# Second branch's operand loaded in the first three dilated items, minimum over key halves by one operand, last memory gating behind the last shift

## Chip, cores and metric

The kernel runs on one core of a Trainium2 chip. The metric is the device time of one execution in microseconds. Five engines work side by side: PE (TensorE: matmuls and transposes), DVE (VectorE), ACT (ScalarE), POOL (GpSimd) and SP (SyncE, whose queue issues most DMAs). Each engine takes its instructions in the order in which they stand in its queue; they wait for one another by semaphores.

## What is computed

One encoder block over 1024 tokens of 1024 channels, in fp32. Three mixers work on the normalised input `h` and are gated, projected and merged:

```python
def reference(x, mem, g_pre, w_in, ...):
    h = rms_norm(x, g_pre[layer])
    a_qkv, bq, bk, bv, mq, ga, gb, gm, mg = jnp.split(h @ w_in[layer], split_at, axis=-1)
    ...
    for gi, (window, dil) in enumerate(((128, 1), (512, 4), (2048, 16))):
        o_g, lse_g = dilated_window_attention(aq[:, :, hs], ak[:, :, hs], av[:, :, hs], window, dil)
        ...
    wts = jax.nn.softmax(jnp.stack(lses, axis=0), axis=0).astype(dt)
    oa = jnp.einsum('gbsh,gbshd->bshd', wts, jnp.stack(outs, axis=0)).reshape(b, s, BRANCH_WIDTH)
    ...
    sc = jnp.einsum('bqkgd,bskd->bkgqs', qc, kb_).astype(jnp.float32) * (HEAD_DIM ** -0.5)
    p = jax.nn.softmax(sc, axis=-1).astype(vb_.dtype)
    ...
    ya = (oa * jax.nn.silu(ga)) @ w_br_a[layer]
    yb = (ob * jax.nn.silu(gb)) @ w_br_b[layer]
    ym = (om * jax.nn.silu(gm)) @ w_br_m[layer]
    merged = gates[:, :, 0] * ya + gates[:, :, 1] * yb + gates[:, :, 2] * ym
    out = merged @ w_out[layer]
    x = x + rms_norm(out, g_post[layer])
```

Branch a is the dilated window attention (4 head pairs by 3 dilations), branch b the grouped-query attention over all keys, branch m the attention into a memory of 256 rows. "The second branch" is b.

## The kernel before

**Operands in two parts.** Most products are made from a high and a low part of each operand: ACT copies the high part into a reduced format (`fp32r`), DVE or POOL subtracts it from the source for the low part, and PE makes three matmuls for each pair of tiles (high by high, high by low, low by high).

**Stages.** (1) Projections and the memory attention, until about 219 us. (2) The second branch's attention, `b_att`, until about 464 us, woven with the projections of the gates. (3) Values, queries, keys, gates and merge factors of the first branch, one run of matmuls without a break on PE, until about 1064 us. (4) The dilated attention, until about 1277 us, woven with the branch projections. (5) The last branch projections and the output product, until the end.

**Order.** `weave` lets two generators take turns by their costs in time: the projections (`run_items`) and the attention. PE's order is as written throughout. In stage 2 the other engines are ordered by a scheduler, by priorities and its own estimates; `tc.issue_after(x)` keeps an instruction behind `x` on its engine. From stage 3 on ACT, DVE, POOL and SP too run in the order in which the code is written.

**Stage 2.** Step `n` of `b_att` makes a `row_max` (line 787: the scores of 128 queries with half of the keys; line 788: their minimum, as the scores stand negated), four heads by two key halves for each item `i`. After the eighth, line 790 takes the minimum over the two halves into `nmt`; `shift` (lines 795 and 796) transposes it on PE and writes it on DVE into four rows of the low query operand `QL`, from where the matmul of line 806 subtracts it from the scores. `scores` follows (lines 805, 806; the exponential on ACT in line 808; the sum over keys on POOL in lines 810 and 812), then `pv` (line 821). `memory_load` and `memory_gate` bring four tiles of the memory branch's result and multiply them by their gates (line 770, two instructions of 512 columns a tile); the table `MEMORY` gives the steps, `fp["last"]` is the latest minimum of line 788. The 128 steps with a `row_max` end at n = 127.

**Stage 4.** Twelve items: `n = 3 p + g`, p the head pair, g the dilation. `visit(b)` for b = 0 to 3 issues the scores of two blocks of 128 queries (lines 1582 and 1589), their softmax (DVE line 1601, ACT line 1602), the transposes, and the products with the values `avs` and `avp` of the item before (lines 1654 and 1661). `rest(T)` for T = 0 to 7 follows with smaller work. In it, `combining` merges the three dilations of a head pair by their log-denominators: `cpt` is fetched, weights are made and stored (line 1818), loaded again in the full shape as `wgt` (line 1788), and POOL multiplies (`weigh`, line 1826), adds (line 1824) and gates (line 1829). `tokens` prepares the operand of the second branch: `b_load(k)` loads the gated result, 128 channels by 1024 tokens, 512 KB, into the tile `bl` (line 1854, SP), `b_high` copies half of it into `bh` (line 1858, ACT), `b_low` subtracts on POOL (line 1862, in place).

The other generator runs the steps `m` = 0 to 15 of the branch projections, `add_y`: 0 to 7 for the memory branch, 8 to 15 for the second branch, whose matmuls (line 1891) read `bh` and `bl`. The weights of a step come by `y_load` (line 1354) into `wr` and are split by `y_split` into one tile, high part in its first half on ACT (line 1359), low part in the second on POOL or DVE (line 1360). PE uses the low part in every third matmul of a step. Steps 16 to 23, of the first branch, come in stage 5 (line 2033, sixteen to eighteen in turns of two, one and one of the four operand parts); the weights of 16 to 18 are split at the end of stage 4, and `third(0)` and `third(1)` there finish the fourth operand part: DVE lines 1977 and 1978, POOL line 1979, ACT line 1869, POOL line 1872.

## Time and profile before

| | us |
|---|---|
| three runs | 1403.37, 1407.81, 1410.76 |
| median | 1407.81 |
| the profiled execution | 1409.11 |
| its span, first to last instruction | 1407.3 |
| mean granted clock of PE | 0.994 of full speed |

The profile has the busy time of each engine, and each instruction with its start, its length, the idle time before it and what ended that. Rows of the timeline read: start in us, length in us, engine, line, operation, what it writes from what it reads, shape, count, and in brackets the idle time before it and its releaser. A `q` behind an engine's name is its queue. PE's matmuls overlap: one of 512 columns is shown with about 0.40 us, while the next starts 0.23 us after it, so PE's lost time is read from the starts.

### The profile page before, as it was taken

What the parts mean: (1) busy time and instruction counts of PE and PEld (TensorE: products, weight loads), DVE (VectorE), ACT (ScalarE), POOL (GpSimd) and SP (SyncE); (2) the same over time, 40 slices, a digit from 0 to 9 for tenths busy, and PEclk for the clock granted to TensorE, in tenths of its full rate; (3) what the DMA queues carried; (4) which work ended last, traced back from release to release, by engine and by line L of the source; (5) the groups of instructions that cost most, each with busy time, mean ns of one, the idle gap of its engine ahead of it and who ended that gap; (6) DMA issues with size and microseconds to landing.
All of it is one profiled execution on the core that took longest, in us unless ns stands there. A gap on an engine that the chain in (4) does not pass through costs nothing.

```text
span 1407.3 us, 21847 instructions
## 1 busy us (share of the span) xinstructions
PE 1381.3 (98%) x7775; PEld 1108.0 (79%) x7775; DVE 1021.6 (73%) x1824; ACT 658.8 (47%) x1384; POOL 579.7 (41%) x444
## 2 busy tenths in 40 slices
PE   7999999999999999999999999999999998999997
PEld 7799986666655789988888888888887786777886
DVE  7768677767776597776777776677787565677977
ACT  6544455666555345333333333343336665653332
POOL 0407702675666100244555554456551143652003
PEclk9999999999999999999999999999999999999999
DMA  6355522322243688424323333333346575876455
GB/s 236 100 180 209 188 105 92 104 90 76 77 138 129 215 258 250 143 83 136 97 95 107 112 120 106 108 117 120 112 132 238 184 212 171 234 222 213 151 195 179
DMA packets 121933, 212.30 MB, mean 151 GB/s; under 512 B 32512, under 2 KB 61024, under 8 KB 121824
## 3 DMA queue, kind: packets, MB, share of 16 engines
q1 hardware_dynamic: 112512, 196.98, 44.0%
q10 hardware_dynamic: 9312, 13.93, 2.7%
q8 instruction: 61, 1.00, 0.3%
q14 instruction: 48, 0.39, 0.1%
HBM read 144.48 MB, written 66.38 MB: 150 GB/s over the span
## 4 chain that ended last, share of the span: by engine, by line
PE 88%; DVE 3%; POOL 2%; ACT 2%; DMA 2%; issue 1%; SPq 0%; DVEq 0%; POOLq 0%; ACTq 0%
PE s L1326 34%; PE d L1891 6%; PE s L1236 4%; PE s L2115 4%; PE ov L821 3%; PE d L147 3%; PE d L145 3%; PE d L149 3%; PE s L1287 3%; PE sc L2033 3%; PE s L1589 2%; PE tr L1661 2%; PE s L806 2%; PE s L805 2%; PE tr L787 2%; PE d L2115 2%
## 5 line engine op out<-in xcount | busy, mean ns | idle before, releaser
L812 POOL TENSOR_TENSOR bl<-bl,bp 128x512 f32<-128x512 f32 x96 | 132.5, 1380 | 54.2 <-ACT bp L808 48.8
L1326 PE MATMUL s<-hh,vS 128*128 128x512 f32 x400 | 133.4, 395 | 0.0
L1326 PE MATMUL s<-vA,vS 128*128 128x512 f32 x450 | 106.6, 390 | 0.0
L1601 DVE CUSTOM_DVE_ANT_0 pra<-s,mask 128x192 f32<-128x192 f32 (+2 forms) x192 | 52.9, 326 | 69.9 <-PE s L1589 41.7
L108 DVE TENSOR_TENSOR vS<-vot,vS 128x512 fp32r<-128x512 f32 x75 | 86.3, 1152 | 19.9 <-ACT vS L107 19.9
L1326 PEld LDWEIGHTS s<-vA,vS 128*128 128x128 f32 x450 | 84.5, 188 | 18.3
L808 ACT ACTIVATE bp<-s 128x512 f32<-128x512 f32 x128 | 75.8, 596 | 45.7 <-PE s L806 44.6
L788 DVE TENSOR_REDUCE bn<-tr 128x1 f32<-128x512 f32 x128 | 84.6, 682 | 11.0 <-PE tr L787 10.0
L145 PE MATMUL d<-hh,wh 128*128 128x512 f32 x224 | 90.1, 402 | 2.4 <-DVE fth L218 2.4
L1602 ACT ACTIVATE pra<-pra,sts 128x192 f32<-128x192 f32 (+2 forms) x176 | 75.1, 429 | 36.9 <-DVE sts L1601 35.5
L149 PE MATMUL d<-hh,wl 128*128 128x512 f32 x224 | 90.0, 402 | 0.0
L147 PE MATMUL d<-hl,wh 128*128 128x512 f32 x224 | 89.5, 400 | 0.0
L1326 PEld LDWEIGHTS s<-hh,vS 128*128 128x128 f32 x400 | 75.3, 188 | 17.7
L1326 PE MATMUL s<-hl,vS 128*128 128x512 f32 x200 | 79.1, 395 | 0.0
L1326 PE MATMUL s<-hh,wh 128*128 128x512 f32 x200 | 78.4, 392 | 0.0
L1326 PE MATMUL s<-hh,wl 128*128 128x512 f32 x200 | 78.4, 392 | 0.0
L1326 PE MATMUL s<-hl,wh 128*128 128x512 f32 x200 | 77.8, 389 | 0.0
L1330 ACT ACTIVATE vv<-s 128x512 f32<-128x512 f32 x50 | 30.0, 599 | 85.6 <-PE s L1326 59.1
L1070 POOL TENSOR_TENSOR vot<-wr 128x512 f32<-128x512 f32 x13 | 22.2, 1706 | 111.9 <-DVE vv L1206 111.9
L821 PE MATMUL ov<-bp,VS 128*64 128x512 f32 x256 | 58.5, 598 | 0.0
L1070 POOL TENSOR_TENSOR vot<-vot,vA 128x512 f32<-128x512 f32 x12 | 19.3, 1608 | 90.6 <-DVE vS L108 90.6
L145 PEld LDWEIGHTS d<-hh,wh 128*128 128x128 f32 x224 | 42.6, 190 | 16.2 <-issue 5.5
(629 smaller groups left out, 4058.9 us busy)
## 6 DMA issues: line engine op xcount, KB each, us to landing
wr<-in_wu SPq DMA_DIRECT2D x40, 512.0 KB
vA<-in_wu SPq DMA_DIRECT2D x24, 512.0 KB
qkd<-ko SPq DMA_DIRECT2D x96, 128.0 KB
wl<-thd SPq DMA_DIRECT2D x24, 512.0 KB
wos<-os SPq DMA_DIRECT2D x12, 512.0 KB
wr<-in_wbr SPq DMA_DIRECT2D x24, 256.0 KB
aq<-qkd SPq DMA_DIRECT2D x12, 512.0 KB
ak<-qkd SPq DMA_DIRECT2D x12, 512.0 KB
```

The costliest lines, as they stand in the source:

```text
L108: V.tensor_tensor(dst_l, src, dst_h.bitcast(F32), op=OP.subtract)
L145: PE.matmul(dst, wh[:, k, :], hh[k][:, t], start=k == 0, stop=False)
L147: PE.matmul(dst, wh[:, k, :], hl[k][:, t], start=False, stop=False)
L149: PE.matmul(dst, wl[:, k, :], hh[k][:, t], start=False, stop=k == 7)
L788: fp["last"] = V.tensor_reduce(st[i]["n"][:, j, c:c + 1], s, axis=AX.X, op=OP.min)
L808: A.activation(pp, s, AF.Exp, scale=-1.0)
L812: G.tensor_tensor(lsum[i % 2], lsum[i % 2], pp, op=OP.add)
L821: PE.matmul(o[e * 64:e * 64 + 64], VS[:, kt, kv], d.pop(kt), start=kt < 2, stop=kt >= NT - 2)
L1326: PE.matmul(BANK[n, c], a, b, start=k == 0 and q == 0 and not more, stop=k == 3 and q == 2, skip_group_check=c in "XW")
L1602: A.activation(src, src, AF.Exp, scale=-1.0, bias=bias, accum_out=sts[:, 1, h, T:T + 1])
L1891: PE.matmul(ps_, a, b, start=k == 0 and q == 0, stop=k == 3 and q == 2)
L2115: PE.matmul(dst[:, e[0]:e[1]], a, b, start=k == 0 and q == 0, stop=k == 3 and q == 2)
```

## The change

Four edits. (1) The four `b_load` move from the items 1 to 4, T = 6, to (item, T) = (0, 2), (0, 6), (1, 3) and (2, 3), and `b_high` and `b_low` from the items 2 to 5 to the items 1 to 4. (2) Line 790 becomes a reduction over the last axis of one operand of 4 by 2 elements. (3) The gatings of the memory tiles 2 and 3 move in the table from the steps 129 to 134 to 139 to 143, and must stand behind the latest shift, not the latest minimum. (4) The split of the weights of step 18 moves from the end of the stage's code to just ahead of `third(0)`.

```diff
         def memory_gate(k, j):
             o, g = [x[j] for x in MT[k]]
-            with tc.issue_after(fp["last"].ins):
+            with tc.issue_after(fp["last" if k < 2 else "shift"].ins):
                 V.scalar_tensor_tensor(o, o, 0.5, g, op0=OP.mult, op1=OP.mult)
             nc.sync.dma_start(od[2, k, :, half[j]], o)
 
         MEMORY = {108: (0,), 110: (1,), 115: (0, 0), 117: (0, 1), 119: (1, 0), 121: (1, 1), 122: (2,), 124: (3,),
-                  129: (2, 0), 130: (2, 1), 133: (3, 0), 134: (3, 1)}
+                  139: (2, 0), 140: (2, 1), 142: (3, 0), 143: (3, 1)}
...
                 if x == 7:
-                    V.tensor_tensor(nmt[i % 2][:, 64:68], st[i]["n"][:, :, 0], st[i]["n"][:, :, 1], op=OP.min)
+                    V.tensor_reduce(nmt[i % 2][:, 64:68], st[i]["n"], axis=AX.X, op=OP.min)
...
-                V.tensor_tensor(QQ[T][1][64:68, 4 * kv:4 * kv + 4], tp[64:68, 0:1, :].to_broadcast([4, 4, 128]),
+                fp["shift"] = V.tensor_tensor(QQ[T][1][64:68, 4 * kv:4 * kv + 4], tp[64:68, 0:1, :].to_broadcast([4, 4, 128]),
                                 ident[64:68, 64:68, None].to_broadcast([4, 4, 128]), op=OP.mult)
...
-                if 2 <= n <= 5 and 4 <= T <= 6:
-                    (lambda: b_high(n - 2, lo), lambda: b_high(n - 2, hi), lambda: b_low(n - 2))[T - 4]()
-                if 1 <= n < 5 and T == 6:
-                    b_load(n - 1)
+                if 1 <= n <= 4 and 4 <= T <= 6:
+                    (lambda: b_high(n - 1, lo), lambda: b_high(n - 1, hi), lambda: b_low(n - 1))[T - 4]()
+                if (n, T) in ((0, 2), (0, 6), (1, 3), (2, 3)):
+                    b_load(((0, 2), (0, 6), (1, 3), (2, 3)).index((n, T)))
...
-                    (lambda: third(0), 2500.0), (lambda: third(1), 2500.0)]
+                    (lambda: [y_split(18, V, qk.tile([P, S], R, name="aq", bufs=2)), third(0)], 2500.0),
+                    (lambda: third(1), 2500.0)]
...
         while pend:
             pend.pop(0)()
-        y_split(18, V, qk.tile([P, S], R, name="aq", bufs=2))
         y_load(19)
```

How instructions move, at three places. POOL in the dilated stage, from the second to the fifth item; the numbers behind `bl_` are the four tiles of the operand, and `og` and `wgt` belong to the merging of the first head pair:

```order
-L1360 TENSOR_TENSOR wh<-wr,wh 128x512 x3
+L1360 TENSOR_TENSOR wh<-wr,wh 128x512 x2
 L1862 TENSOR_TENSOR bl_9733<-bl_9733,bh_9729 128x1024
 L1360 TENSOR_TENSOR wh<-wr,wh 128x512
 L1862 TENSOR_TENSOR bl_9734<-bl_9734,bh_9730 128x1024
 L1360 TENSOR_TENSOR wh<-wr,wh 128x512
-L1826 TENSOR_TENSOR og<-og,wgt 128x1024
 L1862 TENSOR_TENSOR bl_9735<-bl_9735,bh_9731 128x1024
+L1360 TENSOR_TENSOR wh<-wr,wh 128x512
+L1826 TENSOR_TENSOR og<-og,wgt 128x1024
+L1862 TENSOR_TENSOR bl_9736<-bl_9736,bh_9732 128x1024
```

Each subtraction stands one split of weights earlier; that of the last tile, which stood between the gating of line 1829 and the split of step 8, now stands between the two first products with `wgt`.

DVE at the end of the second branch's attention, around the last minimum and the last shift (`tx` and `tb` are the memory tiles 2 and 3):

```order
 L788 TENSOR_REDUCE bn_4659<-tr 128x1 x2
-L770 SCALAR_TENSOR_TENSOR tx_4689<-tx_4689,tx_4690 128x512
-L790 TENSOR_TENSOR bnm_2698<-bn_4659 128x4
-L770 SCALAR_TENSOR_TENSOR tx_4689<-tx_4689,tx_4690 128x512
+L790 TENSOR_REDUCE bnm_2698<-bn_4659 128x4
+L796 TENSOR_TENSOR QL<-tr,cs 4x512
+L770 SCALAR_TENSOR_TENSOR tx_4689<-tx_4689,tx_4690 128x512 x2
 L770 SCALAR_TENSOR_TENSOR tb_4716<-tb_4716,tb_4718 128x512
-L796 TENSOR_TENSOR QL<-tr,cs 4x512
 L770 SCALAR_TENSOR_TENSOR tb_4717<-tb_4717,tb_4719 128x512
```

One gating stood ahead of the minimum and two more ahead of the shift; now all four stand behind the shift.

ACT some 40 us earlier in the same stage, where the last query tile is copied out of its transposes (`QH`), the exponentials `bp` are taken, and the sum over keys is copied as `blh`:

```order
 L808 ACTIVATE bp<-s_4410 128x512
 L808 ACTIVATE bp<-s_4422 128x512
-L107 ACTIVATE blh<-bl_2695 128x512
 L715 ACTIVATE QH<-tr 64x4x128
 L716 ACTIVATE QH<-tr 64x4x128
```

The copy of the sum leaves its place ahead of the four copies of the query tile and goes behind the last of them; it is the scheduler's choice. PE's order is the same in both kernels.

## Prediction

> **What bounds the kernel now.** I read the page first, then the stretches of the dilated stage side by side, then PE's rows wherever two starts lie further apart than the matmul between them needs.
>
> ```profile
> span 1407.3 us, 21847 instructions
> PE 1381.3 (98%) x7775; PEld 1108.0 (79%) x7775; DVE 1021.6 (73%) x1824; ACT 658.8 (47%) x1384; POOL 579.7 (41%) x444
> ```
>
> PE works for nearly the whole span, so no edit helps that only makes another engine cheaper; the change leaves PE's instructions and their order as they are. What is left to win is the time in which PE stands still, and it lies in few places. The first is seen when three stretches of equal work (484, 483 and 484 recorded matmuls; three dilated items each) are set beside each other. The columns are the stretch, its length and each engine's busy time, then the granted clock, the DMA share and GB/s.
>
> ```profile
> 1084.35:1130.33 45.98, 45.98 (x484) 36.60 (x482) 28.16 (x127) 30.27 (x112) 8.64 (x5) 1.00 0.57 182
> 1130.33:1183.07 52.74, 48.76 (x483) 38.58 (x482) 28.12 (x130) 31.13 (x114) 25.48 (x12) 0.94 0.74 202
> 1183.07:1229.47 46.40, 46.30 (x484) 36.48 (x482) 31.61 (x136) 29.51 (x111) 21.52 (x10) 1.00 0.74 208
> 1173.21:1180.04 6.83, 5.07 (x21) 4.25 (x22) 1.96 (x10) 1.87 (x7) 1.71 (x2) 0.50 0.65 179
> ```
>
> The middle one is 6.8 us longer than the first and 6.3 us longer than the third, and its clock fell to 0.50 for 6.83 us. PE's and POOL's rows there say why.
>
> ```profile
> 1170.75 0.40 PE L1891 MATMUL d<-bl,wh 128*128 128x512 f32 x1
> 1174.97 0.80 PE L1891 MATMUL d<-bh,wh 128*128 128x512 f32 x1 [3.82 <-POOL wh L1360]
> 1163.55 2.94 POOL L1826 TENSOR_TENSOR og<-og,wgt 128x1024 f32<-128x1024 f32 x1 [6.90 <-DMA wgt<-wgd]
> 1166.57 2.36 POOL L1824 TENSOR_TENSOR og<-og 128x1024 f32<-128x1024 f32 x1
> 1169.00 2.39 POOL L1829 TENSOR_TENSOR og<-og,wgt 128x1024 f32<-128x1024 f32 x1
> 1171.35 2.35 POOL L1862 TENSOR_TENSOR bl<-bl,bh 128x1024 fp32r<-128x1024 f32 x1
> 1173.65 1.27 POOL L1360 TENSOR_TENSOR wh<-wr,wh 128x512 fp32r<-128x512 f32 x1
> ```
>
> PE's first product with the second branch's operand (step m = 8) needs the low part of its weights, which POOL makes last in a row of five. That row began when the weights `wgt` landed; its fourth member is b_low(3), one of the instructions that the change moves.
>
> **The change part by part: the operand.** Four loads of 512 KB (line 1854), eight ACT copies (line 1858) and four POOL subtractions (line 1862) go one item ahead, the loads up to an item and a half. Their number stays. b_low(3) alone stood in front of something that PE waited for: without it line 1360 starts where line 1862 did, 1171.35 instead of 1173.65, and ends 2.3 us earlier, at 1172.6. PE is ready at 1170.75 + 0.23 = 1170.98 (0.23 is the distance of two 512-column matmuls in the rows below). That alone would leave a wait of 1.7 us. The rest depends on when the row begins, and there the load comes in:
>
> ```profile
> 1147.89 0.32 SPq L1854 DMA_DIRECT2D bl<-od  x1
> 1152.12 1.10 SPq L1788 DMA_DIRECT2D wgt<-wgd  x2
> 1146.50:1163.50 17.00, 17.00 (x211) 13.21 (x209) 8.39 (x50) 11.43 (x45) 10.15 (x5) 1.00 0.93 230
> ```
>
> The load of b_load(3) was issued 4.2 us ahead of `wgt`, in a stretch in which the DMA engines were 93% busy at 230 GB/s. `wgt` took 11 us to release POOL because it stood behind a backlog. 0.52 MB less in front of it are 2.3 us at that rate, so POOL should begin near 1161.3, and line 1360 should end near 1170.3, 0.7 us before PE asks. The third stretch shows such a row without a line 1862 in it:
>
> ```profile
> 1213.00 2.91 POOL L1826 TENSOR_TENSOR og<-og,wgt 128x1024 f32<-128x1024 f32 x1 [4.85 <-DMA wgt<-wgd]
> 1220.78 1.28 POOL L1360 TENSOR_TENSOR wh<-wr,wh 128x512 fp32r<-128x512 f32 x1
> ```
>
> It begins 29.9 us into its stretch (the middle one's 33.2), ends 39.0 us in, and PE is busy for 46.30 of 46.40 us. I take the third stretch as the middle one's new length: **6.3 us**. Upper bound 6.8 (the first stretch), lower bound 4.6 (the wait of 1.7 stays).
>
> What it adds lies beside other work. In the first item the loads meet POOL busy for 8.64 of 45.98 us and DMA at 0.57; the two copies and the subtraction that enter the second item displace nothing on PE's path, as they did not in the first stretch, which held two such sets. If that cover were gone, a copy of 0.6 us would delay an exponential of line 1602 by as much, and PE's transposes behind it.
>
> **The minimum and the gating.** In the second branch's attention (until about 464) PE waits for DVE at the end.
>
> ```profile
> 439.69 0.80 DVE L770 SCALAR_TENSOR_TENSOR tx<-tx,tx 128x512 f32<-128x512 f32 x1
> 440.42 1.24 DVE L790 TENSOR_TENSOR bnm<-bn 128x4 f32<-128x4 f32 x1
> 442.19 1.78 DVE L770 SCALAR_TENSOR_TENSOR tb<-tb,tb 128x512 f32<-128x512 f32 x1
> 444.00 0.69 DVE L796 TENSOR_TENSOR QL<-tr,cs 4x512 fp32r<-4x512 f32 x1
> 440.29 7.87 POOL L812 TENSOR_TENSOR bl<-bl,bp 128x512 f32<-128x512 f32 x5 [0.34 <-ACT bp L808]
> 440.97 0.39 PE L145 MATMUL d<-hh,wh 128*128 128x512 f32 x1
> 441.72 0.30 PE L795 MATMUL tr<-cs,bnm 128*68 128x128 f32 x1 [0.36 <-DVE bnm L790]
> 443.50 0.40 PE L805 MATMUL s<-QH,KS 128*128 128x512 f32 x1
> 444.75 0.50 PE L806 MATMUL s<-QL,KB 68*128 68x512 f32 x1 [0.85 <-DVE QL L796]
> ```
>
> The transpose of line 795 starts 0.75 us after the matmul ahead of it, 0.52 more than 0.23; the scores of line 806 start 1.25 after theirs, 1.02 more. The first waits for the minimum, which took 1.24 us for 4 columns while POOL was adding; the second for the shift, behind three gatings. The change takes the last two tiles' gatings out of this path and lets them follow the shift. They then fill DVE to about 446, where nothing of PE waits for it; their stores to DRAM are read only by the merge, hundreds of us later.
>
> ```profile
> L790 DVE TENSOR_TENSOR bnm<-bn x16: 142/164/1249, 228.5 to 440.4; 128x4 f32<-128x4 f32 x16
> L1940 DVE TENSOR_REDUCE cds<-s x1: 208/208/208, 1263.1 to 1263.1; 128x16 f32<-128x48 f32 x1
> 426.89 0.40 PE L787 MATMUL tr<-KS,QH 128*128 128x512 f32 x1
> 427.52 0.30 PE L795 MATMUL tr<-cs,bnm 128*68 128x128 f32 x1 [0.24 <-DVE bn L788]
> ```
>
> The three numbers of a group are the least, the median and the longest in ns. The minimum takes 0.14 to 0.16 us in half of its 16 runs, and up to 1.25. One of the long ones set DVE back ahead of 427.52, at 0.40 us of PE. No row shows a reduction of 8 columns; the nearest are its own short runs (0.142) and, from above, the reduction of 48 columns of line 1940, 0.21 us. I take 0.16 and expect it free of the stretching.
>
> [...]
>
> Sum here 0.52 + 1.02 + 0.40 = **1.9 us**. Below it: 0, if the next row on DVE takes each place over. Above it: the scheduler also puts one copy `blh` behind the copies of the last query tile.
>
> ```profile
> 403.18 0.63 ACT L107 ACTIVATE blh<-bl 128x512 fp32r<-128x512 f32 x1 [3.88 <-POOL bl L812]
> 408.14 0.39 PE L149 MATMUL d<-hh,wl 128*128 128x512 f32 x1
> 408.79 0.48 PE L787 MATMUL tr<-KS,QH 128*128 128x512 f32 x1 [0.26 <-DVE QL L719]
> ```
>
> ACT stood 3.88 us before that copy with the query copies behind it, and PE's row came 0.65 after the one ahead, 0.42 too late. With the copies first this goes: **0.4 us**, bounds 0 and 0.4.
>
> **The split of step 18.** It stood at the end of ACT's and DVE's queues in this stage:
>
> ```profile
> 1281.50 0.63 ACT L1869 ACTIVATE hh<-og 128x512 fp32r<-128x512 f32 x1 [2.66 <-POOL og L1979]
> 1282.03 0.61 ACT L1359 ACTIVATE aq<-wr 128x512 fp32r<-128x512 f32 x1
> 1283.04 0.40 PE L2033 MATMUL sc<-hl,aq 128*128 128x512 f32 x1
> 1284.10 0.73 PE L2033 MATMUL sc<-hh,aq 128*128 128x512 f32 x2 [0.67 <-DVE aq L1360]
> ```
>
> 1.06 - 0.23 = 0.83: **0.8 us**. Moved ahead of third(0), ACT waits there for the load and DVE for ACT, and behind DVE stand third's products. They come up to 1.4 us later, and with them the fourth part of the operand, which PE asks for only after three steps with parts 0 to 2 (54 matmuls, 12 us from 1277). Bounds 0 and 1.0.
>
> **Sum.** 6.3 + 1.9 + 0.4 + 0.8 = 9.4 us. The profiled execution took 1409.11 us (span 1407.3 and 1.8 around it): 1399.7. It lies 1.3 above the median of 1407.81, so the median should become **1398.4 us**. All later work is one chain on PE, and the loads behind it are released by PE's progress, so I let the gain pass through.
>
> **Rivals.** (a) *The row on POOL starts no earlier.* For it: nothing shows in which order the 16 engines serve a backlog. Against it: the 93%. PE waits 1.7 us; gain 7.7, 1400.1 us. (b) *The same, and the clock halves again.* In the trace it fell 2.2 us after PE had stopped, and the excess of 6.3 is 4.0 of idling and 2.3 of slow clock. Then the gain is 9.4 - 1.7 - 2.3 = 5.4: 1402.4. [...] (c) *The minimum is stretched as before and only the gating helps.* Gain 9.4 - 0.9 = 8.5 at best, 7.1 with the 1.4 of gating and copy lost to the next DVE row too: 1400.7. (d) *Slower: SP stands at the first b_load.* The load waits for the space of the closed stage's tiles, and SP's queue is in order; behind it stand the values that PE uses at 1091.35.
>
> ```profile
> 1074.82 0.42 SPq L1536 DMA_DIRECT2D avs<-vdr  x1
> SPq L1490 <- DMA thd<-wl: 8.3, 1, 8.3
> ```
>
> There are 16.5 us between; SP would have to stand longer before PE loses anything, and 26 us before the gain is gone (a stand of 30: 1412). The longest seen is 8.3, and PE's last use of that space is over by 1064, so 3%.
>
> **How the numbers follow.** Forecast 73%, (a) 12%, (b) 5%, (c) 5%, (d) 3%, and 2% for something unseen on the slow side. The runs of before spread from 1403.37 to 1410.76, so 4.4 us below the forecast, 1394.0, is the low end, and the smallest sum of the bounds (4.6 of gain), 1403.2, the high one; this leaves out (d) and the tails, about 2 in 10. What this kernel's measurement tells from no change is about 0.5%, 7.0 us, so faster means under 1400.8: nearly nine tenths of the forecast, half of (a) and (c), a third of (b): 76%. Within it 18%, slower 6%.
>
> **What would show it.** Right: the stretch of the middle three items 46 to 46.5 us long, no clock of 0.50 between 1160 and 1190, line 1360 done before PE's third product; line 790 under 0.3 us in all 16 runs; no wait of line 806 on QL at the end of the attention; no wait of line 2033 on line 1360. Wrong: line 1826 still released by `wgt` 33 us into its stretch, a new wait of PE on `avs`, `aq` or line 1641 in the first four items, or the gain of the attention given back before 464.

## The result and the profile after

The changed kernel took 1399.27 us (median of 6 runs, 1397.33 to 1401.00), the kernel before 1408.76 us beside it (6 runs, 1403.37 to 1410.76). The ratio on record, which is taken over the runs and is not the quotient of the two medians, is 0.9939, 95% interval 0.9918 to 0.9959, so 8.6 us less (5.8 to 11.6); the medians lie 9.5 us apart. Measured again later, the two came out at 1398.04 us (6 runs) and 1407.61 us (23 runs): 0.9943 (0.9929 to 0.9957), 8.0 us less (6.1 to 10.0), with the medians 9.6 apart. The prediction was 1398.4 us. The gains of the experiments below are worked out from such ratios too, unless medians are named.

The profiled execution took 1401.0 us, the longest of its six. The page of the changed kernel begins with its span:

```profile
span 1399.2 us, 21844 instructions
```

The same stretches as in the prediction, now of the changed kernel, with the rest of the dilated stage and the last stage behind them. For these two I add the kernel before. Columns: the stretch, its length and each engine's busy time, the granted clock, the DMA share and GB/s. After:

```profile
1080.75:1126.74 45.99, 45.99 (x484) 36.59 (x482) 28.11 (x127) 31.36 (x114) 11.02 (x6) 1.00 0.64 198
1126.74:1172.69 45.95, 45.95 (x484) 36.50 (x482) 27.94 (x130) 30.10 (x112) 23.04 (x11) 1.00 0.70 192
1172.69:1219.06 46.37, 46.25 (x483) 36.48 (x481) 31.60 (x136) 29.55 (x111) 21.65 (x11) 1.00 0.77 225
1219.06:1270.17 51.11, 48.77 (x438) 38.52 (x437) 34.60 (x123) 24.48 (x85) 25.99 (x13) 0.97 0.66 189
1270.17:1391.03 120.86, 120.86 (x541) 99.51 (x539) 100.50 (x144) 40.73 (x85) 16.86 (x24) 1.00 0.54 189
```

Before:

```profile
1229.47:1277.02 47.55, 47.21 (x438) 37.50 (x437) 35.86 (x125) 23.86 (x84) 26.20 (x14) 1.00 0.70 204
1277.02:1399.12 122.10, 121.40 (x540) 99.35 (x539) 99.01 (x142) 41.24 (x86) 16.71 (x24) 1.00 0.54 187
```

Read against each other, the pair of profiles gives this account. The first stretch starts at 1080.75 in place of 1084.35: **3.6 us** were won ahead of it. The middle one is 45.95 in place of 52.74: **6.8**. The third is as it was (46.37, 46.40). The fourth is 51.11 in place of 47.55: **3.6 us lost**, at a clock of 0.97. The last is 120.86 in place of 122.10: **1.2** won. Before rounding these make 8.1, the difference of the spans (1407.3 and 1399.2).

The row on POOL that the prediction followed, after the change:

```profile
1155.70 2.89 POOL L1826 TENSOR_TENSOR og<-og,wgt 128x1024 f32<-128x1024 f32 x1 [2.90 <-DMA wgt<-wgd]
...
1163.47 1.27 POOL L1360 TENSOR_TENSOR wh<-wr,wh 128x512 fp32r<-128x512 f32 x1
1167.02 0.39 PE L1891 MATMUL d<-bh,wh 128*128 128x512 f32 x1
```

The last row is PE's third product of step m = 8. POOL's row begins 29.0 us into its stretch (33.2 before), has four members in place of five, and line 1360 is over at 1164.74, while PE asks 40.3 us into the stretch, at 1167.02. The wait of 3.8 us is gone and so is the half clock behind it.

The second branch's attention, after: the group of line 790 (least, median, longest in ns), one of its runs beside POOL's additions, the last shift, and two rows of PE that frame the stretch.

```profile
L790 DVE TENSOR_REDUCE bnm<-bn x16: 142/161/163, 228.0 to 437.4; 128x4 f32<-128x8 f32 x16
423.59 7.27 POOL L812 TENSOR_TENSOR bl<-bl,bp 128x512 f32<-128x512 f32 x5 [0.34 <-ACT bp L808]
423.72 0.15 DVE L790 TENSOR_REDUCE bnm<-bn 128x4 f32<-128x8 f32 x1
438.95 0.69 DVE L796 TENSOR_TENSOR QL<-tr,cs 4x512 fp32r<-4x512 f32 x1 [1.35 <-PE tr L795]
396.51 0.27 PE L795 MATMUL tr<-cs,bnm 128*68 128x128 f32 x1
459.42 0.39 PE L127 MATMUL tr<-bll,one 128*1 128x512 f32 x1 [0.19 <-DVE bll L108]
```

The same two matmuls before:

```profile
396.94 0.27 PE L795 MATMUL tr<-cs,bnm 128*68 128x128 f32 x1
462.99 0.40 PE L127 MATMUL tr<-bll,one 128*1 128x512 f32 x1
```

Line 790 no longer has a long run (1.249 us was the longest before): at 423.72 it takes 0.15 us inside POOL's additions. The gatings follow the shift, which now waits for PE and not the other way round. From the one matmul to the other it is 62.91 us in place of 66.05: the attention won **3.1 us**. The remaining 0.5 of the 3.6 lies ahead of it (396.51 and 396.94); the same matmul stands at 395.76 to 397.67 in the experiments below, with no link to their edits.

What was lost is one new wait. PE's rows, then SP's, of the changed kernel:

```profile
1250.56 0.40 PE L1891 MATMUL d<-bh,wh 128*128 128x512 f32 x1
1252.77 0.24 PE L1929 MATMUL s<-cs,rows 64*128 64x64 f32 x1 [1.82 <-DMA rows<-std]
1242.07 2.50 SPq L1693 DMA_DIRECT2D std<-sr  x4
1248.94 0.32 SPq L1729 DMA_DIRECT2D rows<-std  x1
1253.00:1257.50 4.50, 4.50 (x28) 3.26 (x29) 3.45 (x12) 0.41 (x2) 2.16 (x1) 0.62 0.36 108
```

The last head pair's log-denominators go to DRAM (`std`, line 1693) and come back in another order (`rows`, line 1729). On SP the load stands behind two loads of values and one of weights and was issued 4.4 us after the last write; of that, SP's row of waits puts 0.4 us on the landing of the writes. PE's transpose of line 1929 then started 2.0 us later than the 0.23 of a matmul would have it (1.82 of it by the row), and the clock fell (0.62 in the mean over the next 4.5 us). In the profile of before the same transpose ran without a wait. Whether the change causes this is one of the questions of the experiments.

### The profile page after: what moved, and what is told of

It is laid out like the page before. It is cut to its first block, busy times and chain, and to the rows that moved or that the text cites. A ratio compares the mean times of both kernels' runs of the same rounds, so it can differ in the third digit from the quotient of the medians.

```text
span 1399.2 us, 21844 instructions
## 1 busy us (share of the span) xinstructions
PE 1375.7 (98%) x7775; PEld 1105.8 (79%) x7775; DVE 1019.9 (73%) x1824; ACT 658.5 (47%) x1384; POOL 579.9 (41%) x444
## 4 chain that ended last, share of the span: by engine, by line
PE 89%; DVE 3%; POOL 2%; DMA 2%; ACT 2%; issue 1%; SPq 0%; DVEq 0%; POOLq 0%; ACTq 0%
PE s L1326 35%; PE d L1891 6%; PE s L1236 4%; PE s L2115 4%; PE ov L821 3%; PE sc L2033 3%; PE s L1287 3%; PE d L147 3%; PE d L145 3%; PE d L149 3%; PE s L1589 2%; PE tr L1661 2%; PE tr L787 2%; PE s L806 2%; PE s L805 2%; PE d L2115 2%
## 5 line engine op out<-in xcount | busy, mean ns | idle before, releaser
L1602 ACT ACTIVATE pra<-pra,sts 128x192 f32<-128x192 f32 (+2 forms) x176 | 75.2, 430 | 31.5 <-DVE sts L1601 31.4
```

Source lines behind the costliest of these rows:

```text
L1602: A.activation(src, src, AF.Exp, scale=-1.0, bias=bias, accum_out=sts[:, 1, h, T:T + 1])
```

## The experiments

### The four edits one by one

**The operand alone.** The kernel before with this:

```diff
-                if 2 <= n <= 5 and 4 <= T <= 6:
-                    (lambda: b_high(n - 2, lo), lambda: b_high(n - 2, hi), lambda: b_low(n - 2))[T - 4]()
-                if 1 <= n < 5 and T == 6:
-                    b_load(n - 1)
+                if 1 <= n <= 4 and 4 <= T <= 6:
+                    (lambda: b_high(n - 1, lo), lambda: b_high(n - 1, hi), lambda: b_low(n - 1))[T - 4]()
+                if (n, T) in ((0, 2), (0, 6), (1, 3), (2, 3)):
+                    b_load(((0, 2), (0, 6), (1, 3), (2, 3)).index((n, T)))
```

> The kernel before with the operand's edit alone (loads, copies and subtractions earlier). Theory: the 4.0 us wait ahead of PE's third product of step m = 8 and the half clock behind it go, so the middle stretch is 46.0 long, as after the whole change (52.74 before), 6.3 to 6.8 us; attention and the last step stay as before (waits at 408 to 445 us there; three waits at L2033). If the wait on `rows` at L1929 (1.99 us and half clock, 3.3 us in the profile of the whole change) belongs to the earlier operand, it is here too and the time is 1405 to 1406; if it comes by chance of the transfers, it is in some runs only and the median is 1402 to 1403. Rival: part of the 6.8 us needs the earlier start that attention's edits give, and a wait over 1 us on L1360 is left.

Measured: 1403.09 us (12 runs, 1401.99 to 1405.43) beside 1406.90 us of before (35 runs, 1402.81 to 1409.60); ratio 0.9981 (0.9970 to 0.9993), 2.7 us (1.0 to 4.2). The middle stretch:

```profile
1129.31:1176.11 46.80, 46.07 (x483) 36.59 (x482) 28.02 (x130) 30.11 (x112) 23.23 (x11) 1.00 0.72 188
1160.22 2.95 POOL L1826 TENSOR_TENSOR og<-og,wgt 128x1024 f32<-128x1024 f32 x1 [4.65 <-DMA wgt<-wgd]
1168.04 1.29 POOL L1360 TENSOR_TENSOR wh<-wr,wh 128x512 fp32r<-128x512 f32 x1
```

PE waits for line 1360 no longer, and no wait on `rows` is there; 0.73 us go to a late load of values. The mechanism holds without attention's edits. Yet the time gives 2.7 us (3.8 between the medians), and the 6.3 of the term lie outside its interval. The median of 1403.09 is just above the 1402 to 1403 expected for that case. The longest runs of before are gone, but the shortest (1402.81) was nearly as short as the shortest here (1401.99).

**The minimum alone.**

```diff
-                    V.tensor_tensor(nmt[i % 2][:, 64:68], st[i]["n"][:, :, 0], st[i]["n"][:, :, 1], op=OP.min)
+                    V.tensor_reduce(nmt[i % 2][:, 64:68], st[i]["n"], axis=AX.X, op=OP.min)
```

> The kernel before with the minimum over key halves by one operand alone. Theory: L790 takes under 0.2 us in all 16 runs (once 1.25 before, x16 0.142/0.164/1.249), of which PE gets about 1.0 us at 441.7 us; with two gatings still at the old places PE's waits at 408.8, 410.0 and 413.7 (1.1 us together) stay. PE is 0.5 to 1.1 us earlier at 464 us than before; the time is 1407.7 to 1408.3. Rival: the 1.25 us came with the gatings about it and not with the form of the operation; then PE gains nothing here and the kernel with the gatings alone gains the whole 3 us.

Measured: 1404.85 us (12 runs), ratio 0.9990 (0.9977 to 1.0002). Two runs of line 790 in the kernel before; then, of this kernel, the two matmuls that frame the attention, a gating and PE's wait for the shift:

```profile
410.59 1.23 DVE L790 TENSOR_TENSOR bnm<-bn 128x4 f32<-128x4 f32 x1
425.62 1.25 DVE L790 TENSOR_TENSOR bnm<-bn 128x4 f32<-128x4 f32 x1
```

```profile
397.00 0.27 PE L795 MATMUL tr<-cs,bnm 128*68 128x128 f32 x1
438.51 1.70 DVE L770 SCALAR_TENSOR_TENSOR tx<-tx,tx 128x512 f32<-128x512 f32 x1
442.68 0.50 PE L806 MATMUL s<-QL,KB 68*128 68x512 f32 x1 [1.41 <-DVE QL L796]
460.92 0.39 PE L127 MATMUL tr<-bll,one 128*1 128x512 f32 x1
```

The attention takes 63.92 us, 2.1 less than before. (In the five profiles of kernels without an edit of the attention, these two matmuls are 66.05 to 66.09 us apart, so 0.1 us counts here.) I expected 0.5 to 1.1 at 464 us. The rival, that the gatings made the minimum long, is refuted: the gatings stand at their old places and all 16 runs of line 790 take 0.14 to 0.16 us. The minimum had been long three times (410.59, 425.62, and 440.42, quoted in the prediction), not at the one place that I had priced. PE's waits at 408 to 414 us went here and not with the gatings below; ACT's copy of the sum has its new place in this kernel already, so these runs can't part what the copy gave from what the minimum gave.

At the end of the attention the minimum alone gains nothing. The gating behind it now takes 1.70 us while POOL adds (0.68 before), the next one 1.77 (1.78 before), and the wait for the shift is 1.57 us, where the waits for the minimum and the shift had been 0.52 and 1.02.

**The gatings alone.**

```diff
-            with tc.issue_after(fp["last"].ins):
+            with tc.issue_after(fp["last" if k < 2 else "shift"].ins):
...
-                  129: (2, 0), 130: (2, 1), 133: (3, 0), 134: (3, 1)}
+                  139: (2, 0), 140: (2, 1), 142: (3, 0), 143: (3, 1)}
...
-                V.tensor_tensor(QQ[T][1][64:68, 4 * kv:4 * kv + 4], tp[64:68, 0:1, :].to_broadcast([4, 4, 128]),
+                fp["shift"] = V.tensor_tensor(QQ[T][1][64:68, 4 * kv:4 * kv + 4], tp[64:68, 0:1, :].to_broadcast([4, 4, 128]),
```

> The kernel before with the last four gatings behind the last shift alone. Theory: PE's waits of 0.42, 0.21 and 0.41 us at 408.8, 410.0 and 413.7 and those at 427.5 go, and 444.75's 1.02 too; the minimum at 440 us no longer meets a gating but still meets POOL's adds, so L790 still has a run over 0.5 us. PE is 1.5 to 2.5 us earlier at 464 us. Rival: without the one-operand minimum nothing stays, since L790 grows by what the gatings gave; then PE is under 1 us earlier at 464 us.

Measured: 1407.27 us (12 runs), ratio 1.0000 (0.9988 to 1.0011).

```profile
397.12 0.27 PE L795 MATMUL tr<-cs,bnm 128*68 128x128 f32 x1
462.18 0.39 PE L127 MATMUL tr<-bll,one 128*1 128x512 f32 x1 [0.20 <-DVE bll L108]
```

By time nothing is gained that can be told from none. The attention takes 65.06 us, 1.0 less than before, in place of the 1.5 to 2.5 expected; the rival had put it under 1. The waits at 408, 413 and 427 us are all still there: the theory had given the gatings what belongs to the minimum and to ACT's copy. At the end, however, both waits are gone. Without a gating ahead of it, the last minimum, still in its old form, runs at 440.00, before POOL's next addition at 440.48, and takes 0.17 us.

**The split of step 18 alone.** `y_split(18, ...)` goes from the end of the stage into the lambda of `third(0)`, as in the change.

> The kernel before with the split of step 18 ahead of third(0) alone. Theory: the three waits at L2033 go and PE gains 0.8 to 1.1 us between 1266 and 1292 us; nothing else changes; the time is 1407.5 to 1408. Rival: the split takes 1.2 us of DVE ahead of the last shares' products and DL's copies come late: a new wait at the end takes it back and the time is 1409.

Measured: 1405.28 us (12 runs), ratio 0.9992 (0.9981 to 1.0003). The last stage of this kernel:

```profile
1275.24:1396.08 120.84, 120.84 (x540) 99.49 (x539) 100.26 (x144) 40.71 (x85) 16.88 (x24) 1.00 0.55 189
1259.39 0.24 PE L1929 MATMUL s<-cs,rows 64*128 64x64 f32 x1 [0.73 <-DMA rows<-std]
```

120.84 us, against 122.10: 1.26 us, a little over the range given. A row of PE before shows what was missed, smaller steps around the one of 0.83:

```profile
1282.70 0.50 PE L2033 MATMUL sc<-hh,aq 128*128 128x512 f32 x1
```

It came 0.42 us after the one ahead (1282.28), and the next, at the 1283.04 of the prediction, 0.34 after it, in place of 0.23 each. The second row of the kernel with the split answers the question from above: a wait on `rows` is here too, with the operand at its old place. So is one in the kernel with the gatings alone (0.71 us).

### What the wait in the middle stretch is made of

These profiles brought something that one profile could not show. In none of the last three is the operand moved, and PE's wait at step m = 8 was 3.8 us in before's profile, 0.5 with the minimum alone, 2.3 with the gatings alone and 2.3 with the split alone:

```profile
1170.11 0.51 PE L1891 MATMUL d<-bh,wh 128*128 128x512 f32 x1 [0.51 <-POOL wh L1360]
1172.83 0.50 PE L1891 MATMUL d<-bh,wh 128*128 128x512 f32 x1 [2.33 <-POOL wh L1360]
1173.15 0.49 PE L1891 MATMUL d<-bh,wh 128*128 128x512 f32 x1 [2.27 <-POOL wh L1360]
```

The row's members take the same time in each; what differs is when `wgt` lands. The gatings alone have a middle stretch of 50.15 us; those of the minimum and of the split, with the clock behind POOL's column:

```profile
1129.16:1175.89 46.73, 46.22 (x484) 36.50 (x482) 27.93 (x130) 31.05 (x114) 25.40 (x12) 1.00 0.75 212
1130.45:1180.52 50.07, 47.80 (x483) 37.94 (x481) 28.11 (x130) 31.14 (x114) 25.55 (x12) 0.97 0.75 208
```

Before's 52.74 us is the longest of four. The next two kernels take the operand's edit apart.

**The loads early, copies and subtraction at the old place**, so that POOL's row keeps its five members:

```diff
-                if 1 <= n < 5 and T == 6:
-                    b_load(n - 1)
+                if (n, T) in ((0, 2), (0, 6), (1, 3), (2, 3)):
+                    b_load(((0, 2), (0, 6), (1, 3), (2, 3)).index((n, T)))
```

> The kernel before with the four loads (L1854) early, but the copies and the subtraction in the old items, so that POOL's row is as before, with L1862 in it. The prediction's theory: 0.52 MB less ahead of `wgt` bring the row's start 2.3 us forward (33.2 to 30.9 us into the stretch) and a wait of 1.7 us is left. Rival: the load has no clear part in it and `wgt` lands between 29.5 and 33.2 us by chance, as in the profiles with the load at its old place (33.2, 31.3, 31.2, 29.5); then the wait is anything from 0.5 to 4 us and the median within 1 us of before.

Measured: 1403.62 us (11 runs, 1402.28 to 1407.40) beside 1407.61 us of before (23 runs); ratio 0.9976 (0.9965 to 0.9987), 3.4 us (1.8 to 4.9).

```profile
1130.39:1176.75 46.36, 46.21 (x484) 36.50 (x482) 28.02 (x130) 31.02 (x114) 25.40 (x12) 1.00 0.71 192
1170.98 0.49 PE L1891 MATMUL d<-bh,wh 128*128 128x512 f32 x1 [0.15 <-POOL wh L1360]
```

The row began at 1159.52, 29.1 us into the stretch, and the wait was 0.15 us, with line 1862 still in the row: less than the 1.7 that the prediction's theory left, and less than the 0.5 to 4 of the rival, whose median within 1 us of before is refuted by the interval. By time, the loads alone give as much as the whole edit (3.4 against 2.7 us, intervals that overlap widely).

**The last subtraction on DVE, the load late:**

```diff
-            G.tensor_tensor(l, l.bitcast(F32), h.bitcast(F32), op=OP.subtract)
+            (V if k == 3 else G).tensor_tensor(l, l.bitcast(F32), h.bitcast(F32), op=OP.subtract)
```

> The kernel before with b_low(3) alone on DVE in place of POOL; the load stays late. Theory: POOL's row is 2.35 us shorter (L1826, L1824, L1829, L1360: 9.05 us from its start to the end of L1360 in place of 11.4), so with a start at 29.5 to 33.2 us PE's wait is 0 to 2.0 us, and the median is 1.5 to 3 us under before, half to all of what the operand's edit gave. Rival: if the load was the half of it, a wait of 1.7 us is left in the middle of the runs and the gain is under 1.5 us; or DVE, now 1 us later in its row, lets PE wait at another place.

Measured: 1404.90 us (12 runs, 1403.50 to 1409.68), ratio 0.9988 (0.9978 to 0.9998), 1.7 us (0.3 to 3.1; the expected 1.5 to 3 can't be told from less).

```profile
1162.34 2.94 POOL L1826 TENSOR_TENSOR og<-og,wgt 128x1024 f32<-128x1024 f32 x1 [5.70 <-DMA wgt<-wgd]
```

The row began 31.7 us into the stretch, and PE waited 0.46 us for line 1360, where the expectation had 0 to 2.0; a late load of values made the stretch 47.60 us long all the same. Put together, the row's start in the profiles: 33.2, 29.5, 31.3, 31.2 and 31.7 with the load late, 30.9, 29.0, 29.1 with it early (the operand's edit, the changed kernel, the loads alone), and 29.0, 30.7, 29.1, 28.6, 30.2 in the later kernels with it early. The means are 31.4 and 29.6: moving the loads is worth 1.8 us of start (standard error 0.7), where I had worked out 2.3, with a scatter of 1 to 2 us about both. POOL's 2.35 us are the margin on top. Each half alone gains time by an interval clear of zero; its one profile (0.15 and 0.46 us of wait) would not show that, since one of the four with neither half had 0.51. Both together take the wait away in all seven profiles that have both.

### The changed kernel again, and its new wait

**The changed kernel, unaltered.**

> The changed kernel again, unaltered. Theory (chance of the transfers): before's wait at PE's third product of step m = 8 was 3.99, 2.50, 2.43 and 0.67 us in four profiles of kernels with the operand unmoved, and none in two with it moved; so the middle stretch is 45.9 to 46.8 us here once more, while the wait on `rows` (L1929; 1.99 us in one profile of this kernel, 0.9 in two others, none in three) may be there or not. The median is 1398.5 to 1399.5, and against the mean of before (about 1406.8) the change is worth 7 to 8 us, not 9.5. Rival: the change is worth 9.5 us also here (ratio 0.9933).

Measured: the 1398.04 us from above; five runs from 1397.44 to 1398.64 and one of 1402.50. That one was profiled (the second row is a window that begins 0.3 us before the end of the wait):

```profile
1254.28 0.24 PE L1929 MATMUL s<-cs,rows 64*128 64x64 f32 x1 [3.17 <-DMA rows<-std]
1254.00:1259.00 5.00, 4.72 (x28) 3.54 (x30) 3.08 (x12) 0.41 (x2) 2.90 (x2) 0.66 0.42 141
```

The middle stretch was 45.94 us, as expected. The gain of 8.0 us is at the end of the 7 to 8 expected, but the median is under the range given, and the medians lie 9.6 us apart, as the rival had it. The wait on `rows` has grown to 3.2 us and stands in the long run. In the profiles of kernels with `rows` asked for at the same place it was 0 in five (before, the operand alone, the minimum alone, the subtraction on DVE, and the changed kernel with the old gatings below) and 0.7 to 3.2 in five (the gatings alone, the split alone, the loads alone, and the changed kernel twice). Both sets hold kernels with the operand at its old and at its new place. Five profiles a side can't exclude that the change makes it more frequent; that the change is needed for it is refuted. Its length may be another matter: the three waits over 1 us (1.57, 1.82, 3.17) all stand in kernels with the loads early, the two of 0.7 in kernels with them late.

The traces show what decides it. In the five profiles without the wait SP issued the load of `rows` 2.4 to 2.9 us ahead of line 1929. In the five with it, SP issued the load 0.5 to 2.1 us before PE was ready, and line 1929 started 2.5 to 3.9 us after the issue. So when SP reaches the load, behind its loads of values and weights, counts as much as how long the load takes. No run moves it on SP alone.

**`rows` asked for later.** The last four steps `shares_3` one place later:

```diff
-                    out.append((lambda b=b: shares_3(b), 0.5 * LAST_PAD))
+                    out += [(lambda s=s: shares_3(s), 0.5 * LAST_PAD) for s in ((), (0,), (1,), (2, 3))[b]]
```

> The changed kernel with the last shares' four steps (shares_3) one place later, so that PE asks for `rows` (L1929) about 1.0 us later: two transposes and three products come in between. Theory: the wait at L1929 becomes 1.0 us shorter where it is over that and goes where it is less; with it goes the half clock behind it. The median is 0.5 to 1.5 us under the changed kernel's in the same call, and the longest runs (over 1400) get rarer. Rival: the steps behind (the product with `parts` at L1949, `wide`, the last copies) come later too and a wait there takes it back: no difference or slower.

Measured: 1398.41 us (6 runs, 1397.16 to 1399.75), ratio to before 0.9941 (0.9929 to 0.9953). No wait at line 1929 in its profile, and no run over 1400, but the median is not below the 1398.04 of the changed kernel. The expected 0.5 to 1.5 us did not show. With one long run in six, there was little for the median to gain.

**One load behind `rows`.** The gate of the third head pair (line 1833) is issued behind the load of `rows` in place of ahead of the writes it waits for.

```diff
-                        nc.sync.dma_start(rows[32 * j:32 * j + 32], std[3, j].rearrange("s h (t a) -> (s h t) a", t=NT))
+                        nc.sync.dma_start(rows[32 * j:32 * j + 32], std[3, j].rearrange("s h (t a) -> (s h t) a", t=NT)), (DL.pop("late") if j else int)()
...
-                    lambda: weigh(1, True), lambda: load(2), load_gate, lambda: weigh(2), lambda: weigh(2, True), gate, store]
+                    lambda: weigh(1, True), lambda: load(2), load_gate if p_ < 2 else lambda: DL.update(late=load_gate), lambda: weigh(2), lambda: weigh(2, True), gate, store]
```

> The changed kernel with one load of 512 KB (the gate of the third head pair, L1833) issued behind the load of `rows` in place of ahead of the writes of `std` that `rows` waits for. Theory: what stands in the DMA queues ahead of the writes makes `rows` late (the writes landed 4.2 us after the last was issued, `rows` 3.7 us after its own issue), so `rows` comes about 2 us earlier and PE has no wait over 0.5 us at L1929; POOL's gating at L1829 may wait for its load instead, which PE need not feel. The median is that of the changed kernel (1398 to 1399.3), the longest run under 1400. Rival: the latency of the two transfers and not the queue makes it; a wait of 1 us or more is there as often as before, or POOL, now late, lets PE wait for the third head pair's operand.

Measured: 1398.79 us (5 runs, 1398.63 to 1399.61), ratio 0.9937 (0.9923 to 0.9950). No wait on `rows`. That decides nothing: the load of `rows` was issued at 1248.88, as in the changed kernel's first profile (1248.94), while PE came to line 1929 2.1 us later than there, and the kernel with the old gatings has the old order and no wait either. PE was late because the third stretch, ahead of the edited place, was 48.15 us long:

```profile
1172.91:1221.06 48.15, 46.55 (x484) 36.40 (x482) 31.70 (x136) 29.19 (x111) 22.01 (x11) 1.00 0.75 216
1214.35 0.73 PE L1891 MATMUL d<-bh,wh 128*128 128x512 f32 x2 [1.48 <-POOL wh L1360]
```

It is the wait of the middle stretch over again, one head pair later, where the change moved nothing: line 1826 began at 1205.24, released by `wgt`, 3.4 us later in the stretch than in the changed kernel's first profile, and line 1360 stood behind it in POOL's queue.

### The attention's end

**The gatings at their old place** in the changed kernel.

> The changed kernel with the last four gatings at their old place. Theory: a wait of about 1.5 us of PE for QL (L796) is back near 440.9 us (1.58 in the kernel with the minimum alone), and the wait for `bll` at 459 us (0.36) goes, since PE comes later: PE is 1.2 to 1.6 us later at 464 us than in the changed kernel, and the median is 1399.3 to 1400.5. Rival: the additions' end bounds this stretch and the gatings' move is worth under 0.5 us.

Measured: 1399.78 us (5 runs, 1399.12 to 1400.60), ratio 0.9942 (0.9927 to 0.9958).

```profile
397.21 0.27 PE L795 MATMUL tr<-cs,bnm 128*68 128x128 f32 x1
442.90 0.50 PE L806 MATMUL s<-QL,KB 68*128 68x512 f32 x1 [1.41 <-DVE QL L796]
461.16 0.40 PE L127 MATMUL tr<-bll,one 128*1 128x512 f32 x1
```

The wait for the shift is back at 1.57 us beyond a matmul (441.10 to 442.90 less 0.23), the attention takes 63.95 us: the gatings' move is worth 1.0 (62.91), a little under the 1.2 to 1.6 expected; the median lies in the range given. Of the 1.6 that it takes from the shift, 0.5 are given back behind.

**Where they are given back.** The kernel with `shares_3` later and with the last block's last three additions on DVE:

```diff
-                    G.tensor_tensor(lsum[i % 2], lsum[i % 2], pp, op=OP.add)
+                    (V if i == 15 and kt > 4 else G).tensor_tensor(lsum[i % 2], lsum[i % 2], pp, op=OP.add)
```

> The changed kernel with shares_3 one place later, as before, and with the last three additions of the last block's sum in the second branch's attention on DVE (idle there from 450 to 458.7 us) in place of POOL. Theory: PE's wait of 0.36 us for `bll` at 459 us goes, since an addition takes DVE 0.7 us and POOL 1.3; the gatings, which end at 446, are not the cause of that wait. PE is 0.3 to 0.4 us earlier at 464 us than in the changed kernel; the median is 1397.5 to 1398.4. Rival: what PE waits for there are the exponentials and not the additions, and nothing changes at 464 us.

```profile
396.54 0.27 PE L795 MATMUL tr<-cs,bnm 128*68 128x128 f32 x1
459.10 0.39 PE L127 MATMUL tr<-bll,one 128*1 128x512 f32 x1
```

62.56 us in place of 62.91, as expected: POOL's additions bound the end of this stage once DVE is out of the way. The median of 1398.12 us (5 runs, 1397.10 to 1399.44), ratio 0.9931 (0.9916 to 0.9945), can't be told from the changed kernel's. In its profile 0.8 us were lost again in the next stage, where PE waited twice for low parts made by DVE (0.5 and 0.3 us, lines 1236 and 1287).

### Line 1360 ahead of the row

The last kernel takes up the third stretch. On top of the one just described, the last four steps of the combination of the first two head pairs come one or two steps later, so that POOL makes the weights' low part first:

```diff
-                while todo and T == STEP_T[-len(todo)]:
+                while todo and T == {5: 9, 6: 0, 8: 7}.get(seq.index(it["key"]) if len(todo) < 5 else 0, STEP_T[-len(todo)]):
```

> The kernel e9_both, with the last four steps of the combination of the first and second head pair (L1826, L1824, L1829 and the store) one or two steps later, so that on POOL the low part of the weights (L1360), whose inputs are there 30 us into the stretch, stands ahead of the row that waits for `wgt` and no longer behind it; in the second stretch the store leaves the way of two loads on SP as well. Theory: what made the waits of 0.7 to 4 us was only that L1360 stood behind `wgt` in POOL's order; now PE waits for L1360 in neither stretch, however late `wgt` lands (L1826 30 to 33 us into the stretch), the second stretch is 45.9 to 46.2 us and the third 46.4 long, and the median is 1397.0 to 1398.2 with no run over 1399.5. Rival: POOL's row, now 1.3 us or more later, lets another engine or the next pair's combination come late, and the time is that of the changed kernel or more (1399 to 1401).

Measured: 1398.38 us (5 runs, 1397.12 to 1399.77), ratio 0.9933 (0.9920 to 0.9947).

```profile
1156.43 1.26 POOL L1360 TENSOR_TENSOR wh<-wr,wh 128x512 fp32r<-128x512 f32 x1 [3.04 <-ACT wh L1359]
1217.96 0.44 PE L1661 MATMUL tr<-app,avs 128*64 128x128 f32 x4 [0.61 <-DMA avs<-vdr]
```

Line 1360 now waits for ACT and not for `wgt`; in the middle stretch (45.94 us) it is done 9 us before PE asks. In the third PE does not wait for it either, but 0.61 us for a load of values, the larger part of what makes it 47.23 us and not the 46.4 expected. The order does what it should in this one profile; a gain over the changed kernel is not measurable, the median is just over the 1397.0 to 1398.2 expected, and one run was over the 1399.5 expected at most.

## Why the prediction was right

The time was hit, and most waits were where they had been put and went for the reason given. That the sum of 9.4 us came so near is in part luck: the largest term was 2.6 us too large against the mean of the profiles, the two others together 1.3 us too small, and the rest is within what the measurement can't part (8.0 and 8.6 us by the ratios, 9.5 and 9.6 between the medians).

| term | predicted | shown by the experiments |
|---|---|---|
| operand, middle stretch | 6.3 (4.6 to 6.8) | 6.8 in the profiled pair; 3.7 in the mean of the profiles |
| minimum, gatings and ACT's copy | 2.3 | 3.1: minimum with copy 2.1, gatings 1.0 |
| split of step 18 | 0.8 (0 to 1.0) | 1.2 to 1.3 |
| sum | 9.4 | 8.1 |

The 3.7 is the mean of the four stretches without the operand's edit (52.74, 46.73, 50.15, 50.07: 49.92) less that of the seven with all of it and POOL's row in the change's order (46.80, 45.95, 45.94, 46.65, 45.95, 46.07, 45.94, in the order of the runs above with the changed kernel's two profiles second and third: 46.19). Its standard error is about 1.2 us, from the scatter of the four. It lies under the lower bound of 4.6 that the prediction gave the term. The operand's edit alone, by time, was 2.7 us (1.0 to 4.2). By time the four edits alone add up to 5.2 us (2.7, 1.4, 0.0 and 1.1, each with some 1.5 to 1.8 either way), by medians to 7.1, beside 8.0 to 8.6 and 9.5 to 9.6 of the whole. That the terms add up is shown only within these widths.

**The operand.** The mechanism was right in both halves: `wgt` behind the loads (1.8 us by the means), and line 1862 ahead of line 1360. The margin predicted, line 1360 done 0.7 us before PE asks, was 2.3 us in the changed kernel's profile and 0.25 with the operand alone (1168.04 + 1.29 = 1169.33, and 1129.31 + 40.27 = 1169.58): of the right size, within the scatter of `wgt`. What failed is the size of the term, "I take the third stretch as the middle one's new length": the new length was right within 0.5 us, but it was set against the one old length that the profile of before showed, the longest of four. The 6.3 us hold a wait that other profiles of the same POOL order had with 0.5 to 2.3 us. The runs of before said as much: 1403.37 beside 1410.76 is a scatter of 7 us, while the changed kernel's six lie within 3.7.

**The attention.** "One of the long ones set DVE back ahead of 427.52": I had counted two long runs of line 790 and there were three; the one at 410.59 was left out, and the row of the group with its three numbers did not tell how many there were. The waits at the end were also given to the wrong edits, 0.52 us to the minimum and 1.02 to the gatings: the gatings alone take both away, while the minimum alone only makes one wait of 1.57 us out of the two. What the minimum gives, it gives before the end. Rival (c), the minimum stretched as before, is refuted by line 790's 142/161/163. That the minimum by one operand would be free of the stretching, on which 0.52 and 0.40 of the sum rest, was my estimate; no run ahead of the result shows it. The changed kernel does, with 0.15 us inside POOL's additions, where the form with two operands had taken 1.23 to 1.25. With the minimum alone the gating that took its place beside the additions took 1.70 us (0.68 before). Why the two-operand form is longer beside the additions and the reduction is not, no run shows.

**The gatings** were worth the 1.0 that stood for them, but not as thought: they take away 1.6 us of waits, of which 0.5 are lost again behind. The 0.36 us for `bll` at 459 us is the new bound behind, on POOL.

**The split** brought 1.2 to 1.3, above the bound of 1.0, by the smaller steps beside the wait that was priced.

**The rivals.** (a) and (b), that POOL's row starts no earlier, fell by the means (29.6 and 31.4 us); single starts overlap, 28.6 to 30.9 beside 29.5 to 33.2. The half clock after a wait of 1.7 us, which (b) adds, was near the edge of what the runs show: it came after a stop of 1.98 us (1250.56 to 1252.77 less 0.23) and not after one of 1.74, both before line 1929. (d), SP standing at the first load, did not come: line 1854 was issued at 1071.18 and no long stand followed. No rival had named the wait on `rows`.

**The gain passed through**, as assumed, except for that wait, which took 3.6 us in the profiled run. Of the two long runs of this kernel, 1401.00 and 1402.50 us, both were profiled and both have it; the ten others, 1397.33 to 1399.61, were not profiled.

## What to carry to other kernels

A wait that a profile shows before a late transfer is one draw from a distribution (0.5 to 3.8 us for the same order here): look at the scatter of the run times first, and if it is as wide as the wait, take the mean over several profiles as the price and not the one that you have. Where an instruction that the bottleneck needs stands behind one that waits for a transfer in an in-order queue, change the order; making the transfer earlier here only changed the odds (a start at 29.6 us in the mean in place of 31.4). (Both took PE's wait away in the middle stretch, and the time did not tell the two apart.) A group's least, median and longest time do not say how often it was long; list the long ones before pricing them. And shortening one of two instructions that wait in a row can be worth nothing there, if the next one is stretched in its place (here 0.14 us in place of 1.24, and 1.70 in place of 0.68 behind it).

## What was unexpected of the hardware

PE's clock fell to half after shorter stops than the one of 3.82 us: after waits of 1.82 and 3.17 us on `rows` (0.62 and 0.66 in the mean over the next 4.5 and 5 us, 0.50 from 1254 to 1257 behind the first) and of 2.27 and 2.33 us on line 1360 (0.97 over the stretch, 0.50 from 1174 to 1176 with the split alone). Behind the waits of 1.57 us on `rows` (the loads alone) and 1.48 us in the third stretch it stayed at 1.00:

```profile
1256.40:1259.80 3.40, 3.36 (x34) 2.58 (x36) 2.37 (x11) 0.41 (x2) 3.40 (x3) 1.00 0.62 230
```

The shortest of the five stops with a lower clock behind them is 1.98 us long (the wait of 1.82); one of 1.74 (the wait of 1.57) had none. What decides it between these two, no run shows. In the middle stretch a wait of 2.27 us so cost up to 4.1 us (50.07 less 45.94, the stretch of the changed kernel).

The landing of one transfer of 512 KB under load (`wgt`, DMA share 0.7 and more) moved by up to 3.7 us against its stretch between profiles with the same order of loads (29.5 to 33.2 us into it), although PE's stretch ahead of the latest was 45.98 us long, as in the changed kernel (45.99). What in the DMA queues decides this, no run here shows.
